# Tuned fp32 layer on one core: token rows split from the transposes' bank, another load order, memory rows in the second block, a reordered first block

## The chip, the cores and the metric

The kernel runs on one core of a Trainium2 chip. The metric is the device time in microseconds of that core. Its engines are named as the profile names them: PE (TensorE, matrix products and transposes), DVE (VectorE), ACT (ScalarE), POOL (GpSimd) and SP (SyncE, which issues the loads).

## The reference

One layer over 512 rows of 1024 numbers and 256 memory rows, all fp32: half a SwiGLU feed-forward, a mixer of three attentions with gates, and another half feed-forward.

```python
x = x + 0.5 * swiglu(rmsnorm(x, ffn1_norm), ffn1_wg, ffn1_wu, ffn1_wd)
h = rmsnorm(x, mix_norm)
aq, ak, av, bq, bk, bv, cq = split(h @ w_in)
o_a = diff_attention(rope(norm(aq)), rope(norm(ak)), av, lam)
o_b = chunk_band_attention(norm(bq), norm(bk), bv, b_rel_bias)
mk, mv = split(rmsnorm(mem, mem_norm) @ w_mem_kv)
o_c = memory_attention(norm(cq), norm(mk), mv)
y = sum over i of sigmoid(h @ w_gate + b_gate)_i * (o_i @ w_branch_i)
x = x + y @ w_out
x = x + 0.5 * swiglu(rmsnorm(x, ffn2_norm), ffn2_wg, ffn2_wu, ffn2_wd)
x = rmsnorm(x, final_norm)
```

D_FF is 2816; the memory attention (branch C) has 4 heads of 128.

## The kernel before

**Arithmetic.** Each fp32 operand is split (`split`, L75 to L78) into a high half, cast by ACT, and a low half, the difference, made by DVE; a product is three matmuls (high by high, low by high, high by low). Weights come by SP into one of six raw buffers ("raw", 128x1024) and are split from there.

**The feed-forward halves** go through the hidden columns in four chunks of 4, 6, 6 and 6 tiles of 128 (`CHUNKS`). Two tiles make an *item*. Gate and up projections of an item are computed by a scheme with seven block products instead of eight: operands on the token side are seven matrices `M[1]` to `M[7]` (split sums and differences of the transposed rows, made by `Operands.rows` and `combine`), on the weight side seven blocks, four of them plain weights or sums `s1` to `s4` of weights (`Item.prep`). A product (`mm7`) is 24 matmuls of 128x256 into an accumulator bank; between products that share a bank, ACT saves it (`snap`), DVE adds the saved part (`plus`, the tiles `cc`), ACT applies the silu (`sg`) and DVE multiplies (`pr`). `run_jobs` goes through a list of jobs; each job's weight block is prepared ahead as far as a ring of blocks has room, and PE runs the jobs in the order of the list, written out by hand. Behind an item's products comes the chunk's down-projection with 128x512 matmuls (L110 to L112): 96 in the first chunk, with the last two products of the chunk behind its first step.

**Rows.** The four row tiles of x are loaded, their mean squares are taken by ACT in two halves, POOL raises them to the power -1/2 (`rs`, L121), DVE scales them by it and by the gain (`xn`, L141), PE transposes eight squares into two "t" banks (L201), ACT copies each bank to a raw buffer (L202), and `combine` forms the operands from it. The 256 memory rows (two tiles `mt`) go the same way to `mT` (`mem_rows`, `norm_T`); in the program they stand ahead of FFN1's last chunk, but the scheduler puts their norms, and the first one's transposes (L149), in the first block.

**Start of the mixer.** The memory keys' product goes into the two "s" banks, then come `norm4` and `heads_T` (transposes of `mk`), the query product, and the memory values' product `mv`, again in the "s" banks. Then the attention steps run by a plan, a string in which `p` is a part of the next projection, `f` a part of the gates' product, `c.qt`, `c.sc`, `c.sc2`, `c.pt`, `c.pv` the steps of the memory attention (query transposes, scores of two pairs of heads, transposed probabilities, product with `mv`). The row maximum `nm` (L754) and the exponentials `p` (L759) stand behind each score; `yb` (L834) is a part of the rotary embedding, from tables that POOL scales (L687, L691), and `hb` (L697) is the gates' bias.

PE's order inside `run_jobs` is written by hand; the other engines' orders are set by the scheduler.

## Time and profile before

| | us |
|---|---|
| median of 3 runs | 1266.1 (1265.81 to 1266.46) |
| profiled execution, own time | 1268.73 |
| span of the profiled execution | 1266.9 |
| PE busy | 1228.1 |
| DVE busy | 843.0 |
| ACT busy | 596.8 |
| POOL busy | 106.2 |

The span is what the trace covers; the execution's own time has 1.8 us more around it. A share of busy time is a mean over the span; the rows below show the stretches apart.

### The profile page before, as it was taken

To read this page: it belongs to the slowest core of one execution; us is meant where nothing else is said; L and a number is where in the kernel's file an instruction comes from. 1 tells how busy PE (TensorE), PEld (TensorE's weight loads), DVE (VectorE), ACT (ScalarE), POOL (GpSimd) and SP (SyncE) were. 2 spreads that over 40 slices of the span, in tenths; PEclk is the share of its full clock that TensorE was granted. 3 is DMA by queue.
4 is the path that set the end of the run, shared out by engine and by line. 5 is a ranking of instruction groups with operands and counts; after the bars stand their busy time and mean duration, and the time that the engine had idled before them with its cause. 6 is when DMAs were issued, how large, how long until landed. Compare 5 with 4: busy or idle time off the path is not lost.

```text
span 1266.9 us, 19640 instructions
## 1 busy us (share of the span) xinstructions
PE 1228.1 (97%) x7808; PEld 1119.2 (88%) x7808; DVE 843.0 (67%) x1377; ACT 596.8 (47%) x1115; POOL 106.2 (8%) x108
## 2 busy tenths in 40 slices
PE   7889999999999899999999999999989999999997
PEld 7779989989987799999999999888887998998996
DVE  7977667667664756667765664554697776766753
ACT  7534525435443455554554544442464452542543
POOL 1100000000000301111121121111000000000002
PEclk8899999999999899999999999999989999999999
DMA  6532423323333413212221321145143242332311
GB/s 222 174 103 82 135 84 107 127 79 122 102 123 117 123 39 109 88 42 84 88 88 54 93 88 38 63 146 186 34 135 115 70 134 97 101 125 76 123 44 67
DMA packets 53084, 127.57 MB, mean 101 GB/s; under 512 B 10112, under 2 KB 10624, under 8 KB 52992
## 3 DMA queue, kind: packets, MB, share of 16 engines
q1 hardware_dynamic: 52416, 125.27, 31.1%
q8 instruction: 61, 1.00, 0.3%
q10 hardware_dynamic: 576, 1.05, 0.2%
q14 instruction: 31, 0.25, 0.1%
HBM read 122.11 MB, written 4.19 MB: 100 GB/s over the span
## 4 chain that ended last, share of the span: by engine, by line
PE 91%; DVE 4%; ACT 1%; DMA 1%; POOL 1%; issue 1%; SPq 0%; POOLq 0%; DVEq 0%; ACTq 0%
PE ps_s L373 19%; PE ps_g L110 9%; PE ps_g L112 9%; PE ps_g L111 9%; PE ps_o L373 5%; PE ps_p L110 5%; PE ps_p L112 5%; PE ps_p L111 4%; PE ps_p L373 4%; PE ps_g L373 4%; PE ps_s L110 3%; PE ps_s L111 3%; PE ps_s L112 3%; PE ps_o L906 2%; PE ps_s L874 2%; PE ps_t L722 1%
## 5 line engine op out<-in xcount | busy, mean ns | idle before, releaser
L77 ACT CAST whi<-wraw 128x1024 fp32r<-128x1024 f32 (+1 forms) x120 | 119.1, 993 | 144.6 <-PE ps_s L373 74.1
L78 DVE TENSOR_TENSOR wlo<-wraw,whi 128x1024 fp32r<-128x1024 f32 (+1 forms) x120 | 137.9, 1151 | 67.8 <-ACT whi L77 65.1
L373 PE MATMUL ps_s<-mhi,whi 128*128 128x256 f32 x496 | 140.3, 283 | 8.1 <-ACT snap L417 7.9
L373 PE MATMUL ps_s<-mlo,whi 128*128 128x256 f32 x496 | 139.3, 281 | 0.0
L373 PE MATMUL ps_s<-mhi,wlo 128*128 128x256 f32 x496 | 138.3, 281 | 0.6 <-DVE wlo L78 0.6
L373 PEld LDWEIGHTS ps_s<-mhi,whi 128*128 128x128 f32 x496 | 94.6, 191 | 10.6 <-ACT snap L417 9.5
L77 ACT CAST whi<-quarter 128x1024 fp32r<-128x1024 f32 x54 | 56.8, 1052 | 96.4 <-PE ps_o L112 22.4
L373 PEld LDWEIGHTS ps_s<-mlo,whi 128*128 128x128 f32 x496 | 94.7, 191 | 0.9 <-DVE mlo L78 0.2
L373 PEld LDWEIGHTS ps_s<-mhi,wlo 128*128 128x128 f32 x496 | 94.5, 191 | 0.9 <-DVE wlo L78 0.8
L110 PE MATMUL ps_p<-whi,hh 128*128 128x384 f32 (+1 forms) x264 | 95.0, 360 | 0.0
L112 PE MATMUL ps_p<-whi,hl 128*128 128x384 f32 (+1 forms) x264 | 89.6, 340 | 0.0
L111 PE MATMUL ps_p<-wlo,hh 128*128 128x384 f32 (+1 forms) x264 | 89.0, 337 | 0.0
L78 DVE TENSOR_TENSOR wlo<-quarter,whi 128x1024 fp32r<-128x1024 f32 x54 | 66.0, 1222 | 23.9 <-ACT whi L77 23.9
L110 PE MATMUL ps_g<-hh,fh 128*128 128x512 f32 x192 | 78.1, 407 | 0.0
L112 PE MATMUL ps_g<-hh,fl 128*128 128x512 f32 x192 | 75.5, 393 | 0.1
L111 PE MATMUL ps_g<-hl,fh 128*128 128x512 f32 x192 | 74.9, 390 | 0.0
L859 DVE CAST kx<-ps_t 128x256 fp32r<-128x256 f32 x32 | 13.6, 425 | 84.6 <-PE ps_t L857 84.6
L121 POOL TENSOR_TENSOR rsh<-msh,mhalf 128x4 f32<-128x4 f32 x38 | 45.2, 1191 | 277.5 <-DVE msh L127 225.8
L78 DVE TENSOR_TENSOR fl<-wraw,fh 128x768 fp32r<-128x768 f32 x48 | 50.0, 1042 | 24.0 <-ACT fh L77 24.0
L77 ACT CAST fh<-wraw 128x768 fp32r<-128x768 f32 x48 | 39.9, 833 | 37.7 <-PE ps_g L111 22.4
L724 ACT COPY pT<-ps_t 128x512 f32<-128x512 f32 (+3 forms) x56 | 23.5, 452 | 69.3 <-PE ps_t L722 69.3
L110 PEld LDWEIGHTS ps_p<-whi,hh 128*128 128x128 f32 x264 | 50.4, 191 | 1.6
(416 smaller groups left out, 3691.7 us busy)
## 6 DMA issues: line engine op xcount, KB each, us to landing
wraw<-in_ffn_w SPq DMA_DIRECT2D x88, 512.0 KB, 3.8
wraw<-in_ffn_wd SPq DMA_DIRECT2D x44, 512.0 KB, 3.9
wraw<-in_w_u SPq DMA_DIRECT2D x32, 384.0 KB, 3.2
wraw<-in_w_gb SPq DMA_DIRECT2D x32, 384.0 KB, 3.1
wraw<-in_w_gf SPq DMA_DIRECT2D x16, 384.0 KB, 3.1
wraw<-in_w_mem_kv SPq DMA_DIRECT2D x8, 512.0 KB, 4.1
wraw<-in_w_out SPq DMA_DIRECT2D x8, 512.0 KB, 4.8
x_sb<-in_x SPq DMA_DIRECT2D x4, 512.0 KB, 7.0
```

Source lines behind the costliest of these rows:

```text
L77: nc.scalar.copy(out=hi, in_=raw)
L78: (engine or nc.vector).tensor_tensor(out=lo, in0=raw, in1=f32(hi), op=ALU.subtract)
L110: nc.tensor.matmul(ps, lhsT=st[0], rhs=mv[0], start=first, stop=False)
L111: nc.tensor.matmul(ps, lhsT=st[0], rhs=mv[1], start=False, stop=False)
L112: return nc.tensor.matmul(ps, lhsT=st[1], rhs=mv[0], start=False, stop=last)
L121: nc.gpsimd.tensor_tensor(out=rs, in0=ms, in1=mhalf[:, :n], op=ALU.pow)
L373: nc.tensor.matmul(ps[:, c], lhsT=x, rhs=y, start=first and j + k + n == 0, stop=k == 3 and n == 2, skip_group_check=True)
L722: nc.tensor.transpose(ps[:, j * P:(j + 1) * P], pt[:, j * P:(j + 1) * P], ident)
L724: nc.scalar.copy(out=pT[:, :n * P], in_=ps[:, :n * P])
L859: nc.vector.tensor_copy(out=un.kx[:, :, qs], in_=heads(p2[:, 0:256], 2))
L874: nc.tensor.matmul(out_, lhsT=q, rhs=k, start=j == 0, stop=j == 1)
L906: nc.tensor.matmul(o[:, vs], lhsT=pT[:, j * P:(j + 1) * P], rhs=un.v[:, j, vs], start=j == 0, stop=j == i)
```

## The change

- x row tile 1 is loaded second, ahead of the gain.
- The first two row tiles' high and low halves are taken from the transposes' bank; ACT's copy to the raw buffer stands behind.
- The mean square of a row is one activation of 1024 instead of two of 512 (`mean_rsqrt` takes either).
- `run_jobs` is called over all chunks, up to the last down-projection half; the second chunk's first product is put behind the first chunk's last two (`hole`). The first block of each feed-forward has another order of products, with the fifth in two halves ("5a", "5b"); `s1`, `s2` and `s4` are made apart, when they are first needed.
- The accumulators of the second half of a down-projection stand in another order.
- The memory rows' loads, squares and norms stand at the end of the second chunk's jobs' list ahead of its down-projection (`mem_norms`, as `middle`), in raw buffers; their transposes stay where `mem_rows` was.
- At the start of the mixer the `mv` product goes into "t" banks, the transposes of `mk` come behind it, and the plan of the first projection tile (`PLAN_C0`) is another one.

```diff
-PLAN_C0 = "p2 c.qt p2 c.sc p2 f4 c.sc2 p3 f2 c.qt f2 c.pt f4 c.pv"
+PLAN_C0 = "p6 c.qt p3 f4 c.sc f4 c.sc2 f2 c.qt f1 c.pt f1 c.pv"
...
-                nc.scalar.copy(out=self.raw[dh][:, :, t * P:(t + 1) * P], in_=k4(ps))
-            self.combine(t)
+                cols = slice(t * P, (t + 1) * P)
+                if t < 2:
+                    split(k4(ps), *(v[:, :, cols] for v in self.M[1 + dh]))
+                nc.scalar.copy(out=self.raw[dh][:, :, cols], in_=k4(ps))
+            if t >= 2:
+                self.combine(t)
...
-        ss = tiny("ss", 2)
-        dump = scratch("sq")
-        for dh in range(2):
-            d = slice(dh * 512, dh * 512 + 512)
-            square_half(src[:, d], dump[:, d], ss[:, dh:dh + 1])
+        ss = tiny("ss", 1)
+        square_half(src, scratch("sq") if dump is None else dump, ss)
...
-        if t == 0:
+        if t == 1:
             gain1 = load_gain("ffn1_norm")
-        elif t < 3:
+        if 0 < t < 3:
             w1_raw.append(load(a["ffn1_w1"][0, t - 1], 1024))
...
+                if self.s1 is None:
+                    self.s1 = quarter()
+                    add(out=self.s1, in0=self.raw(2), in1=self.raw(3), op=ALU.add)
                 if p == 6:
-                    self.s1, self.s2 = quarter(), quarter()
-                    add(out=self.s1, in0=self.raw(2), in1=self.raw(3), op=ALU.add)
+                    self.s2 = quarter()
                     add(out=self.s2, in0=self.s1, in1=self.raw(0), op=ALU.subtract)
...
+                elif p == "5a":
+                    self.z = bank("p" if self.ft // 2 % 2 else "o")
+                    mm7(self.z, blk, 5, True, (0,))
+                elif p == "5b":
+                    mm7(self.z, self.blk5, 5, False, (1,))
...
                 order += [(items[0], 1), (items[0], 2), (items[1], 1), (items[1], 2)]
+                order += [(items[0], "5a"), (items[0], 6), (items[0], "5b"), (items[0], 7), (items[1], 6), (items[0], 4),
+                          (items[0], 3), (items[1], 5), (items[1], 7)]
             else:
-                order += [(items[0], 1), (items[0], 2)]
...
+                if n == 1:
+
+                    jobs.insert(hole, product(items[0], 1))
...
+            if n == 1 and middle:
+                jobs.append(Job(middle, lambda got: None, 0, 0))
...
-                    acc.extend(bank(t) for t in (("g", "g", "s", other) if dh == 0 else ("s", z, "g", "g")))
+                    acc.extend(bank(t) for t in (("g", "g", "s", other) if dh == 0 else (z, "g", "g", "s")))
...
+    def mem_norms():
+
+        gain = load(a["mem_norm"].partition_broadcast(P), 1024)
+        mix_in["mn"] = []
+        for t in range(NMT):
+            mt = load(a["mem"][t * P:(t + 1) * P, :], 1024)
+            xn = scratch("mn")
+            rs = mean_rsqrt(squares(mt, xn))
+            for dh in range(2):
+                norm_half(xn, mt, rs, (gain[:, :512], gain[:, 512:]), dh)
+            mix_in["mn"].append(xn)
...
-        gain = load_gain("mem_norm")
         for t in range(NMT):
-            mt = scratch("mt")
-            nc.sync.dma_start(out=mt, in_=a["mem"][t * P:(t + 1) * P, :])
-            norm_T(mt, squares(mt), gain, mix_in["mT"], t)
+            for dh in range(2):
+                transpose_half(mix_in["mn"][t], *mix_in["mT"], t, dh)
...
-        yn = mem_pool.tile([P, 512], F32, tag="mk", name="mk", bufs=3)
-        sq = mem_pool.tile([P, 512], F32, tag="mk", name="mksq", bufs=3)
-        heads_T(norm4(mk_ps[t], yn, sq, gck), mkT, slice(t * P, (t + 1) * P))
+        yn = mem_pool.tile([P, 512], F32, tag="mk", name="mk", bufs=2)
+        sq = mem_pool.tile([P, 512], F32, tag="mksq", name="mksq", bufs=2)
+        mk.append(norm4(mk_ps[t], yn, sq, gck))
...
-    mv_ps = rows_product([bank("s") for _ in range(NMT)], mT, a["w_mem_kv"], 512, **mem_w)
+    mv_ps = rows_product([bank("t") for _ in range(NMT)], mT, a["w_mem_kv"], 512, **mem_w)
     mv = base.tile([P, NMT, 512], F32, tag="kx", name="mv", bufs=2)
     for t in range(NMT):
         nc.scalar.copy(out=mv[:, t, :], in_=mv_ps[t])
+    for t in range(NMT):
+        heads_T(mk[t], mkT, slice(t * P, (t + 1) * P))
```

The instructions stand in another order on the engines. DVE in FFN1's first block, before the change; `mt` is a memory row tile, `mlo` and `wlo`, `olo`, `flo` are low halves of tokens and of weight blocks, `quarter` a sum of weights, and the last row is the low half of item 1's sixth product's block:

```order
L141 SCALAR_TENSOR_TENSOR xn<-mt,rs,gain 128x512 x2
L78 TENSOR_TENSOR wlo<-quarter,whi 128x1024
L78 TENSOR_TENSOR wlo<-wraw,whi 128x1024
L399 TENSOR_TENSOR quarter<-wraw 128x1024
L78 TENSOR_TENSOR wlo<-quarter,whi 128x1024
L400 TENSOR_TENSOR quarter<-quarter,wraw 128x1024
L409 TENSOR_TENSOR quarter<-wraw 128x1024
L78 TENSOR_TENSOR olo<-quarter,ohi 128x1024
L422 TENSOR_TENSOR cc<-ps_o,snap 128x512
L405 TENSOR_TENSOR quarter<-wraw,quarter 128x1024
L78 TENSOR_TENSOR flo<-quarter,fhi 128x1024
```

DVE at the same place after it; the last row is again the low half of item 1's sixth product's block:

```order
L78 TENSOR_TENSOR flo<-quarter,fhi 128x1024
L243 TENSOR_TENSOR gl<-gl,quarter 128x4x256
L78 TENSOR_TENSOR mlo<-quarter,mhi 128x4x128
L78 TENSOR_TENSOR mlo<-gh,mhi 128x1024
L78 TENSOR_TENSOR wlo<-quarter,whi 128x1024
L442 TENSOR_TENSOR pr<-sg,cc 128x256
L403 TENSOR_TENSOR quarter<-wraw 128x1024
L78 TENSOR_TENSOR mlo<-gl,mhi 128x1024
L406 TENSOR_TENSOR quarter<-quarter,wraw 128x1024
L418 TENSOR_TENSOR quarter<-wraw 128x1024
L414 TENSOR_TENSOR quarter<-wraw,quarter 128x1024
L78 TENSOR_TENSOR wlo<-quarter,whi 128x1024
```

The memory rows' half norms (`xn<-mt`) have gone from this stretch, and item 1's sums of weights (L403, L406) stand just ahead of the block that needs them.

PE in FFN1's first block, before, where products 5 (`ps_o<-mhi,whi`) and 6 (`ps_s<-mhi,ohi`) of item 0 begin, each in its bank; L149 are the transposes of the first memory row:

```order
L373 MATMUL ps_g<-mhi,flo 128x256
L373 MATMUL ps_o<-mhi,whi 128x256
L373 MATMUL ps_s<-mhi,ohi 128x256
L149 MATMUL ps_t<-ident,xn 128x128 x8
L373 MATMUL ps_o<-mlo,whi 128x256
L373 MATMUL ps_o<-mhi,wlo 128x256
L373 MATMUL ps_o<-mhi,whi 128x256
```

PE after, in the second chunk, where the first memory row's transposes (`mn`) stand:

```order
L376 MATMUL ps_p<-mhi,ohi 128x256
L376 MATMUL ps_p<-mlo,ohi 128x256
L376 MATMUL ps_p<-mhi,olo 128x256
L149 MATMUL ps_t<-ident,mn 128x128 x8
L376 MATMUL ps_s<-mhi,whi 128x256
L376 MATMUL ps_s<-mlo,whi 128x256
L376 MATMUL ps_s<-mhi,wlo 128x256
```

The transposes have moved from between two products of the first block to between two products of the second chunk.

DVE at the start of the mixer, before, around the first row maxima of scores (L754):

```order
L78 TENSOR_TENSOR fl<-wraw,fh 128x768
L754 TENSOR_REDUCE nm<-ps_g 128x2
L78 TENSOR_TENSOR fl<-wraw,fh 128x768
L679 TENSOR_SCALAR gb<-gb 128x64
L755 TENSOR_SCALAR nm<-nm 128x2
L754 TENSOR_REDUCE nm<-ps_g 128x2
L697 TENSOR_SCALAR hb<-hb 128x24
L755 TENSOR_SCALAR nm<-nm 128x2
L820 TENSOR_REDUCE hss<-squ 128x4
L834 TENSOR_TENSOR yb<-ps_p,sg 128x4x32 x2
```

DVE there after the change (L793 is the maximum `nm`, L736 `hb`, L873 `yb`, L859 the sum of squares for the rotary part's norm):

```order
L78 TENSOR_TENSOR mkl<-ps_t,mkh 128x4x128
L78 TENSOR_TENSOR cql<-ps_t,cqh 128x512
L736 TENSOR_SCALAR hb<-hb 128x24
L859 TENSOR_REDUCE hss<-squ 128x4
L873 TENSOR_TENSOR yb<-ps_p,sg 128x4x32 x2
L875 TENSOR_TENSOR y_4321<-ps_p,cg 128x256
L127 TENSOR_SCALAR msh<-hss 128x4
L876 TENSOR_TENSOR y_4321<-y_4321,yb 128x256
L879 TENSOR_TENSOR y_4321<-y_4321,rsh 128x256
L883 TENSOR_TENSOR hl_4328<-y_4321,hl_4328 128x4x64
L793 TENSOR_REDUCE nm<-ps_g 128x2
L794 TENSOR_SCALAR nm<-nm 128x2
```

`hb`, the sum of squares, `yb` and the rotary sums have moved from behind the first two maxima to ahead of the first.

## Rows read from the trace of the kernel before

**Rows 1.** The page, part 4: the chain that ended last, shares by engine.

```profile
PE 91%; DVE 4%; ACT 1%; DMA 1%; POOL 1%; issue 1%; SPq 0%; POOLq 0%; DVEq 0%; ACTq 0%
```

**Rows 2.** Waits of PE: what released it, us in total, times, longest.

```profile
PE ps_s L373 <- ACT snap L417: 7.9, 8, 1.5
```

**Rows 3.** Windows: length, busy of PE, PEld, DVE, ACT, POOL, PEclk, DMA share, GB/s.

```profile
40.00:50.00 10.00, 8.46 (x57) 8.05 (x57) 9.56 (x12) 6.29 (x10) 1.39 (x1) 0.84 0.52 173
100.00:150.00 50.00, 50.00 (x427) 49.63 (x426) 37.31 (x44) 27.70 (x39) 0.00 (x0) 1.00 0.36 114
415.00:420.00 5.00, 5.00 (x13) 3.93 (x14) 3.84 (x9) 1.20 (x2) 1.80 (x2) 0.54 0.21 72
```

**Rows 4.** DMA issues at 1.16 and at 1.64 us: count, KB, us to landing.

```profile
gain<-in_ffn_norm SPq DMA_DIRECT2D x1, 512.0 KB, 5.2
x_sb<-in_x SPq DMA_DIRECT2D x1, 512.0 KB, 6.2
```

**Rows 5.** Timeline of DVE, first block: start, duration, line, operation [idle before it].

```profile
23.31 1.22 DVE L78 TENSOR_TENSOR flo<-wraw,fhi 128x1024 fp32r<-128x1024 f32 x1
24.45 0.69 DVE L221 TENSOR_TENSOR quarter<-gl,gh 128x512 f32<-128x512 f32 x1
25.05 1.22 DVE L400 TENSOR_TENSOR quarter<-quarter,wraw 128x1024 f32<-128x1024 f32 x1
...
34.91 1.42 DVE L141 SCALAR_TENSOR_TENSOR xn<-mt,rs,gain 128x512 f32<-128x512 f32 x2 [0.44 <-POOL rs L121]
...
55.45 1.22 DVE L78 TENSOR_TENSOR flo<-quarter,fhi 128x1024 fp32r<-128x1024 f32 x1
```

**Rows 6.** Timeline of POOL, first block.

```profile
9.58 0.55 POOL L121 TENSOR_TENSOR rs<-ms,mhalf 128x1 f32<-128x1 f32 x1 [3.09 <-DVE ms L193]
...
30.02 4.86 POOL L121 TENSOR_TENSOR rs<-ms,mhalf 128x1 f32<-128x1 f32 x1 [9.81 <-DVE ms L156]
```

**Rows 7.** Timeline of PE, first block of FFN1.

```profile
35.81 1.94 PE L149 MATMUL ps_t<-ident,xn 128*128 128x128 f32 x8 [1.23 <-DVE xn L141]
38.12 0.58 PE L373 MATMUL ps_o<-mlo,whi 128*128 128x256 f32 x1 [0.36 <-DVE mlo L78]
...
64.71 0.39 PE L373 MATMUL ps_s<-mhi,whi 128*128 128x256 f32 x1 [1.51 <-ACT snap L417]
64.94 0.28 PE L373 MATMUL ps_s<-mlo,whi 128*128 128x256 f32 x1
...
67.45 0.28 PE L373 MATMUL ps_s<-mhi,wlo 128*128 128x256 f32 x1
...
97.31 0.39 PE L110 MATMUL ps_g<-whi,gh 128*128 128x512 f32 x1
...
97.99 0.28 PE L373 MATMUL ps_s<-mhi,whi 128*128 128x256 f32 x1
```

**Rows 8.** Timeline of PE, start of the mixer.

```profile
414.92 0.77 PE L110 MATMUL ps_s<-mwh,mh 128*128 128x512 f32 x1 [5.78 <-DVE mk L602]
...
438.22 0.39 PE L110 MATMUL ps_g<-mkh,cqh 128*128 128x256 f32 x1 [0.74 <-ACT p L759]
...
450.56 0.34 PE L110 MATMUL ps_p<-whi,hh 128*128 128x384 f32 x1
```

**Rows 9.** Timeline of DVE, start of the mixer.

```profile
424.20 1.21 DVE L78 TENSOR_TENSOR mwl<-wraw,mwh 128x1024 fp32r<-128x1024 f32 x1
...
439.85 0.17 DVE L697 TENSOR_SCALAR hb<-hb 128x24 f32<-128x24 f32 x1
```

**Rows 10.** Timeline of POOL, start of the mixer.

```profile
438.43 0.87 POOL L691 TENSOR_TENSOR sg<-sg,ga 128x128 f32<-128x128 f32 x2
```

**Rows 11.** Timeline of PE, first block of FFN2.

```profile
928.85 0.58 PE L373 MATMUL ps_o<-mlo,whi 128*128 128x256 f32 x1 [3.17 <-DVE mlo L78]
...
986.33 0.28 PE L373 MATMUL ps_s<-mhi,whi 128*128 128x256 f32 x1
```

**Rows 12.** Timeline of DVE, first block of FFN2.

```profile
943.67 1.23 DVE L78 TENSOR_TENSOR flo<-quarter,fhi 128x1024 fp32r<-128x1024 f32 x1
```

More of the change, by code (lines that the diff above doesn't have):

```diff
@@ L362, in block, with mm7 @@
             return weight(None, 1024, fp, (("fhi", "flo"), ("ohi", "olo"))[n - 4], 1, raw=raw)
[L364 to L366 removed]
+        def mm7(ps, blk, m, first, parts=(0, 1)):
+            for j in parts:
                 c = slice(j * HS, (j + 1) * HS)
@@ L435, in done @@
             def done(self, f):
+                if not self.G:
+                    self.G += [fp.tile([P, 6, S], F32R, tag=t, name=t) for t in ("gh", "gl")]
                 split(self.pr[f], *(v[:, self.g0 + f, :] for v in self.G))
@@ L1084, in row_out @@
     def row_out(t, ss):
-        ms = tiny("ms", 1)
-        nc.vector.tensor_scalar(out=ms, in0=ss[:, 0:1], scalar1=EPS, scalar2=ss[:, 1:2], op0=ALU.add, op1=ALU.add)
-        rs = rsqrt(ms)
+        rs = mean_rsqrt(ss)
         xn = scratch("xn")
```

94 lines of the change are left out of this document (50 added, 44 removed).

## The prediction

> **What bounds the kernel now.** I read the page first, then the sum of TensorE's (PE's) waits, then the timelines of the stretches where PE waits. PE is on 91% of the chain that ended last [rows 1], so the reader is to look only for what shortens or lengthens PE's own row of work. Between 100 and 150 us PE is busy 50.00 of 50 [rows 3], and it stays so through the other chunks; its waits lie at three places. One kind is the wait for the snapshot copy, 7.9 us in eight pieces [rows 2], spread over the first blocks of both feed-forward halves. The first block of FFN1 is held by the vector engine (DVE): it works back to back from 20 to 60 us, PE stands at 38.12 for a low half, at 64.71 for a snapshot (1.51), and PE's mark "first product of the next chunk" comes at 97.99 [rows 5, 7]. The start of the mixer has the longest single wait, 5.78 us for `mk`, at 414.92 [rows 8]. The first block of FFN2 has a 3.17 us wait at 928.85, and its mark comes at 986.33 [rows 11]. Each pause is paid twice: after the 5.78 us the granted clock was 0.54 of full speed over 415 to 420, thus near the lower of the two levels (1.2 of 2.4 GHz), and 5 x 0.46 = 2.3 us of PE's work were lost; the 40 to 50 us stretch, with short pauses, shows 0.84, 10 x 0.16 = 1.6 us lost [rows 3]. These two are my prices, 1.6 and 2.3, for one pause of some two us or more.
>
> The profiled execution's span is 1266.9 us and its own time 1268.73; the median of the runs is 1266.1. I add up the terms against the span and put the sum on the median, so 1266.1 plus the sum.
>
> **Unit prices.** A product is 24 matmuls of 128x256; from its second at 64.94 to its last at 67.45 are 22 steps of 0.114, so 2.74 us for a product. A 512-wide matmul of the down-projection takes (97.99 - 97.31) / 3 = 0.227 [rows 7]. On DVE, back to back, a 1024-wide operation takes 24.45 - 23.31 = 1.14, a 512-wide one 0.60 [rows 5], and a 256-wide one, by the same scale, an estimated 0.34.
>
> **Term 1, FFN1's first block: -5.1.** Removed from it: both memory rows' norms, two each of a mean, two half norms (34.91, 1.42) and a 0.44 us wait for POOL in front [rows 5]; DVE does nothing else then. Moved behind it: the second operands of the products that now come later (s2, s4 are computed one at a time), and the order of products, so that DVE comes earlier to the block of item 1's sixth product. Row tile 1 comes second and the gain third: the gain now lands about where x row 1 landed, 1.64 + 6.2 = 7.8, instead of 1.16 + 5.2 = 6.4 [rows 4]. That puts row 0's norm some 1.4 later, but the first two rows' low halves no longer wait for raw copies, and rows 2 and 3 land where they did. I leave the fourth row's norm where it ended before, at 22.1 (the next 1024-wide operation began 1.14 ahead of 23.31). From there the changed order has, up to and with the low half of item 1's sixth product, 19 operations of 1024, eight of 512 and two of 256: 21.6 + 4.8 + 0.7 = 27.1, with 1.1 of idle time while ScalarE casts `ohi`: 50.3. Before, the same low half ended at 55.45 + 1.22 = 56.7 [rows 5]. From there PE has seven products and the down-projection's 96 matmuls ahead of the mark: 7 x 2.74 + 96 x 0.227 = 19.2 + 21.8, so 91.3. The two snapshot waits of 1.5 are not among it, because products 4 and 3 of item 0 now lie between the sixth product's snapshot and the next user of its bank. PE has run out of work by about 48.1, so it pauses about two us and I add the lower price of a clock fall, 1.6: 92.9 against 97.99, -5.1. Bounds: without a pause -6.7; if DVE's chain starts 2 us later (the gain holds row 0 and all behind it), -3.
>
> **Term 2, the memory rows in the second block: +1.3.** Their transposes stood in a pause of PE (eight in 1.94 at half clock, at 35.81 [rows 7]) and cost nothing; the work that hid them was DVE's. They now stand in a chunk in which PE never waits: half of 1.94, so +1.0. PE takes them in its order, whether the norm is there or not. On SP's queue a gain and two memory rows come to stand between the `w1` loads and the first `wd` loads of that chunk, in three of the six raw buffers, and the `wd` loads behind them wait for those buffers. By the changed order the norm is ready 13.2 to 14 us after the block's start and PE arrives after 13.6, +0.3. DVE has room, 37.31 of 50 us busy [rows 3]; the norms' own time, 1.42 each, costs nothing by itself. Bounds: +0.8 to +2.5 without the rival below.
>
> A row that speaks against this part: POOL's power operation of one column took 0.55 at 9.58, and 4.86 at 30.02, while DVE worked without a gap [rows 6]. The Trainium skill, "SBUF — State Buffer", section "SBUF: two separate sides", says that a DVE operation with two SBUF inputs and a GpSimd operation that reads SBUF exclude each other for a whole instruction; the row agrees with it in kind. By that rule the moved norm would meet the same lock beside the second chunk's subtractions; it is case (c) below.
>
> **Term 3, start of the mixer: -0.7.** The `mv` product leaves the "s" banks, in which it waited for `mk`, for "t" banks that are free: the 5.78 and the 2.3 lost on the clock go. What is late next, in order: the second pair's low half now stands behind four reductions on DVE (some 1.7); the second `mk` transpose waits for a "t" bank, that is for ScalarE's copy of `mv`, which stands behind a table load (some 1.2, unshown before, bounds 0 and 2); the first query transposes wait for `mkl` (2 to 3.7). Last comes the second score: its bank's exponentials follow the row maximum `nm`, and on DVE `hb` and `yb` now stand ahead of `nm` (before: `nm` first, then `hb` at 439.85 [rows 9]). `hb` and the rope tables are small loads on SP's queue behind the weight loads that wait for the last low half of `mv` (before, the one at 424.20 and one more right behind it [rows 9], 426.6; now some 421.9), so they come 4.7 us earlier: POOL's last table operation, before 438.43 + 0.87 = 439.3 [rows 10], ends at 434.7, and the maxima and exponentials of the first score about 440.0. The second score, before at 438.22, is then at 440; from it to the second projection tile there are 27 matmuls of 512, 384 or 256 columns and 20 transposes, now without the six of a projection and twelve of the gates that the new plan puts earlier: 8.3 us, so 448.3 against 450.56 [rows 8], -2.3. The idle time ahead of the second score costs a clock fall, +1.6. Bounds: +1.5 where two of the new waits fall together, -5.2 where the table chain doesn't bind (8.1 less 1.7 and 1.2).
>
> **Term 4, FFN2's first block: +1.9.** There are no memory rows to take out here. DVE has as much to do; the copies to the raw buffer now follow the subtraction that reads the same bank (0.7 to 1.2 of DVE waits at the third row). By the list the low half of item 1's sixth product is done at 944.95, before at 943.67 + 1.23 = 944.9 [rows 12], but before PE had products 4 and 3 of item 0 to do meanwhile and now it has not: it pauses from about 941.5. Mark: 944.95 + 19.2 + 21.8 = 985.95, and the clock fall at the higher price, 2.3: 988.2 against 986.33, +1.9. Bounds -0.5 (no fall) and +2.5.
>
> **The rest: 0.** The one job list over all chunks, the hole that takes the next chunk's first product into the down-projection, the other order of accumulators and the squares in one activation of 1024 lie where PE has no wait before; PE's work covers them. If that cover fails at one boundary it costs one low half, 1.2.
>
> **Sum.** -5.1 + 1.3 - 0.7 + 1.9 = -2.6: 1263.5 us, -0.21%. A measurement of this kernel can tell some 0.2% (2.5 us) from no change: faster means below 1263.6, slower above 1268.6.
>
> **The rivals.** (a) More gain: the table chain does not bind the second score and the pause at the mixer's start goes whole, term 3 is -5.2, the sum -5.1 + 1.3 - 5.2 + 1.9 = -7.1: 1259.0. For it: `nm` needs only scores; the chain is four engines long and my times for SP and POOL are placed by hand. Against: `hb` and `yb` stand ahead of `nm` in DVE's order. (b) No change, the first block does not do what it is written to do: row 1 second delays the gain, the DVE list starts 2 us late, term 1 is -3, and a new wait makes term 3 +0.5: -3 + 1.3 + 0.5 + 1.9 = +0.7, 1266.8. (c) Slower: the norm of the first memory row is late in FFN1's second block, because POOL's power operation takes 4.86 instead of 0.55 beside a busy DVE [rows 6]. PE, in order, stands at the transposes for 4.3, and the clock falls: term 2 is 1.3 + 4.3 + 2.3 = 7.9, the sum -5.1 + 7.9 - 0.7 + 1.9 = +4.0, 1270.1. It decides from about 4 us of lateness. For it: the 4.86. Against: DVE has gaps there, a quarter of its time [rows 3].
>
> **How the numbers follow.** Forecast 0.50, spread from 1261 to 1265.5 by its terms' bounds; (a) 0.25; (b) 0.14; (c) 0.11. Of the forecast's 0.50, 0.28 lies below 1263.6. Faster 0.28 + 0.25 = 0.53, same 0.22 + 0.14 = 0.36, slower 0.11. The range leaves out (c) and a small tail of (a): 1257.5 to 1267.5.
>
> **What would show it.** Right: the low half of item 1's sixth product ends near 50, the next chunk's down-projection mark moves by some 5 us, no 5.78 wait at 409 to 415, the wait ahead of the second score names `nm` or an exponential. Wrong: a PE wait of over 1 us for `xn` or `mn` in FFN1's second block; a first product that starts after 18 us; the second projection tile later than 450.6 less what term 1 and 2 gave; any new wait at a chunk boundary.

## Result: 1273.8 us, slower by 0.6%

The changed kernel's median is 1273.82 us over 4 runs (1272.23 to 1275.16), beside 1266.1 over 3 runs of the kernel before: ratio 1.0060 [1.0041, 1.0080]. Forecast were 1263.5, with a range of 1257.5 to 1267.5. The time is outside it and the sign is wrong. A fourth run of the kernel before took 1740.59 us and is left out.

The profiled execution took 1272.23, its span is 1270.3. On the page PE is still nearly the whole chain that ended last (before 91% [rows 1]), with DVE up from the rest. From the section of the page on the chain, shares by engine:

```profile
PE 90%; DVE 6%; ACT 1%; DMA 1%; issue 1%; POOL 0%; SPq 0%; POOLq 0%; DVEq 0%; ACTq 0%
```

The sum of PE's waits in the kernel after (engine, line, what it waited for: us in total, times, longest) against [rows 2]: the snapshot's 7.9 us are no longer at the head; other waits have come instead.

```profile
PE ps_o L376 <- DVE mlo L78: 5.6, 2, 3.6
PE ps_g L110 <- ACT gh L77: 4.0, 2, 2.0
PE ps_t L206 <- ACT gh L210: 3.8, 1, 3.8
```

To see where the time went I cut each trace into six stages, at starts of PE's rows: FFN1's first block up to the next chunk's first product (where that product already stands in the first block's down-projection, 2.72 us are taken off, so 97.40 - 2.72 = 94.7 in the first trace of after); FFN1's second chunk; its third and fourth; from there to FFN2's first transposes (the mixer); FFN2's first block; its three other chunks. The two marks in the first trace of after, each with the product that is taken off in front of it (before: 97.99 [rows 7] and 986.33 [rows 11]):

```profile
97.40 0.28 PE L376 MATMUL ps_g<-mhi,whi 128*128 128x256 f32 x1
991.18 0.28 PE L376 MATMUL ps_g<-mhi,whi 128*128 128x256 f32 x1
```

Two traces of each kernel:

| stage, us | before | before, again | after | after, again | mean difference |
|---|---|---|---|---|---|
| FFN1, first block | 98.0 | 97.2 | 94.7 | 97.0 | -1.8 |
| FFN1, second chunk | 91.05 | 91.05 | 92.6 | 93.05 | +1.8 |
| FFN1, third and fourth | 184.4 | 184.4 | 185.0 | 185.1 | +0.65 |
| mixer | 531.8 | 531.2 | 530.35 | 530.1 | -1.3 |
| FFN2, first block | 81.1 | 80.5 | 85.8 | 85.7 | +4.95 |
| FFN2, other chunks | 273.6 | 273.65 | 275.0 | 275.1 | +1.4 |

The differences sum to +5.7, the spans' own difference (mean 1271.6 against 1265.95). So FFN1's first block gave 1.8 and not 5.1, the mixer 1.3; all the rest lost. A single trace is good to a few us in a first block: g1, g2 and h2 below have PE, DVE and ACT in the same order in FFN2's first block, and their traces have 83.1, 86.3 and 86.9 us for it. FFN1's third and fourth chunk and FFN2's later ones repeat to 0.1.

### The profile page after: what moved, and what is told of

It reads as the page before. It is cut to its first block, busy times and chain, and to the rows that moved or that the text cites. A ratio compares the mean times of both kernels' runs of the same rounds, so it can differ in the third digit from the quotient of the medians.

```text
span 1270.3 us, 19631 instructions
## 1 busy us (share of the span) xinstructions
PE 1230.0 (97%) x7808; PEld 1120.4 (88%) x7808; DVE 845.7 (67%) x1377; ACT 598.3 (47%) x1103; POOL 106.2 (8%) x108
## 4 chain that ended last, share of the span: by engine, by line
PE 90%; DVE 6%; ACT 1%; DMA 1%; issue 1%; POOL 0%; SPq 0%; POOLq 0%; DVEq 0%; ACTq 0%
PE ps_s L376 18%; PE ps_g L110 9%; PE ps_g L112 9%; PE ps_g L111 9%; PE ps_o L376 5%; PE ps_p L110 5%; PE ps_p L112 5%; PE ps_p L111 5%; PE ps_p L376 4%; PE ps_g L376 4%; PE ps_s L112 2%; PE ps_s L110 2%; PE ps_s L111 2%; PE ps_o L945 2%; PE ps_s L913 2%; PE ps_t L761 1%
## 5 line engine op out<-in xcount | busy, mean ns | idle before, releaser
L376 PE MATMUL ps_s<-mlo,whi 128*128 128x256 f32 x512 | 145.4, 284 | 2.1 <-DVE mlo L78 2.1
L376 PE MATMUL ps_s<-mhi,whi 128*128 128x256 f32 x512 | 145.7, 285 | 1.9 <-ACT whi L77 1.6
L376 PE MATMUL ps_s<-mhi,wlo 128*128 128x256 f32 x512 | 145.3, 284 | 2.0 <-DVE wlo L78 2.0
L376 PEld LDWEIGHTS ps_s<-mhi,whi 128*128 128x128 f32 x512 | 99.5, 194 | 2.9 <-ACT whi L77 1.8
L376 PEld LDWEIGHTS ps_s<-mlo,whi 128*128 128x128 f32 x512 | 98.8, 193 | 3.3 <-DVE mlo L78 2.9
L376 PEld LDWEIGHTS ps_s<-mhi,wlo 128*128 128x128 f32 x512 | 99.3, 194 | 2.4 <-DVE wlo L78 2.4
```

The lines of the kernel that those rows point to most:

```text
L376: nc.tensor.matmul(ps[:, c], lhsT=x, rhs=y, start=first and j + k + n == 0, stop=k == 3 and n == 2, skip_group_check=True)
```

## Experiments

Each edit is shown against the kernel named ahead of it. "Ratio" is to the kernel before, in the same set of runs on one chip, with its 95% interval; its own median was 1265.9 to 1267.1 in the five sets, so kernels of different sets are compared by their ratios (0.1% is 1.27 us). The theory at the start was that the changed order of products is at fault, in FFN2's first block above all; the rivals were the hand-fixed list over all chunks, the memory rows' new place, the new mixer start, and the first rows' loads and their split from the bank.

### One part undone in the kernel after

**The same kernel again.**

> The changed kernel once more, beside the kernel before on the same chip. Theory A (the loss lies in FFN2's first block and at the second down-projection step of the first chunks): about +6 to +8 us against before in the median, and the profile again shows FFN2's first block some 4 to 5 us longer than before and a 2.0 us wait for gh in both halves. Rival B (the first trace was an unlucky one, what differs is the number of falls of the granted clock): the trace shows other falls, and the FFN2 block differs from the first trace by over 1.5 us.

1274.77, ratio 1.0059 [1.0044, 1.0074]: the same loss.

**e1: FFN2's first block in the old order.**

```diff
+                if pre == "ffn2":
+                    order += [(items[0], 6), (items[0], 5), (items[0], 7), (items[0], 4), (items[0], 3),
+                              (items[1], 6), (items[1], 5), (items[1], 7)]
+                else:
```

> The changed kernel with FFN2's first block in the order of products of the kernel before (6, 5, 7, 4, 3, 6, 5, 7), all else as changed. Theory A1 (the new order of products is what costs FFN2's block time): 2 to 4 us less than the changed kernel, and the waits at the second item's sixth product (1.6 and 1.7 us) go. Rival A2 (VectorE sets that block's end, TensorE only comes to it earlier, and the order is not the cause): within 1 us of the changed kernel, the waits merely stand elsewhere.

1271.53, ratio 1.0047 [1.0030, 1.0063], not resolved from after's 1.0059. In its trace the block went from 85.8 to 82.7, not to the 80.5 to 81.1 of before; the waits of 1.6 and 1.7 are gone, and one for a low half is now 4.67.

**e2: the first chunks' last two products ahead of the down-projection instead of behind its first step.**

```diff
+                    if n == 0 and dh == 0:
+                        jobs += end
                     for k in range(0, nf, 2):
...
                         if dh == 0 and k == 0:
-                            jobs += end
+                            if n > 0:
+                                jobs += end
```

> The changed kernel with the first chunks' last two products (4 and 3 of the second item) ahead of the down-projection's first step instead of behind it, so that this step and the next chunk's first product both stand between product 3 and the step that reads its result. Theory A: the two waits of 2.0 us for gh go, -3 to -4 us. Rival: the weight blocks of products 4 and 3 come late instead, since they are prepared later than TensorE wants them; the time is within 1 us of the changed kernel and new waits for whi or wlo of 1.5 us or more show.

1270.93, ratio 1.0033 [1.0023, 1.0042], by the ratios 3.3 less than after, as forecast; the two waits for `gh` are gone. First blocks 95.8 and 84.5.

**e7: both edits.**

> The two edits of e1 and e2 together: FFN2's first block in the old order of products, and the first chunks' last two products ahead of the down-projection. If the two causes are apart, their gains add up: 6 to 7 us less than the changed kernel, +0.5 to +1.5 against the kernel before. If VectorE sets FFN2's first block whatever TensorE's order (rival), the second adds only FFN1's half: 4 to 5 us less, +3 against before.

1272.05, ratio 1.0042 [1.0028, 1.0056]: no better than e2 alone. FFN2's block is at 86.1, with PE waits for the snapshot of 2.59 and 1.51 again and one of 5.76 for a low half. The gains don't add here; in the trace other waits stand where those that were taken away had been.

**e4: the old mixer start and plan.** (The old `PLAN_C0`, `mv` in the "s" banks, `heads_T` of each `mk` tile right behind its norm.)

> The changed kernel with the start of the mixer as before (the value product in the s banks, key transposes ahead of it, the old plan of the first projection tile). If the changed start gives what the trace suggests (-1.4 us from the end of the key product to the second projection tile): 1 to 2 us slower than the changed kernel, with the 5.8 us wait back. Rival (the clock fall it now has in another place takes the gain away): the same as the changed kernel within 0.7 us.

1275.64, ratio 1.0069 [1.0054, 1.0084], unresolved from after; in the trace the mixer takes 533.1 instead of 530.1.

**e3: the memory rows back ahead of the last chunk.** They then run in FFN1's first block, as before.

```diff
+        gain = load_gain("mem_norm")
         for t in range(NMT):
-            for dh in range(2):
-                transpose_half(mix_in["mn"][t], *mix_in["mT"], t, dh)
+            mt = scratch("mt")
+            nc.sync.dma_start(out=mt, in_=a["mem"][t * P:(t + 1) * P, :])
+            norm_T(mt, squares(mt), gain, mix_in["mT"], t)
...
-    ffn("ffn1", x_sb, ops, fp, row_mix, raws=w1_raw, before_last=mem_rows, middle=mem_norms)
+    ffn("ffn1", x_sb, ops, fp, row_mix, raws=w1_raw, before_last=mem_rows)
```

> The changed kernel with the memory rows' loads, squares and norms back where they were (the first block decides, as the scheduler puts them), all else as changed. From the traces FFN1's second chunk is 1.6 to 2.0 us longer since the change, while its first block ends 1 to 3 us earlier. Theory (a trade of two about equal sums): within 1 us of the changed kernel; first block 2 to 4 us later, second chunk 1 us shorter, since VectorE sets the first block's end and gets the norms' 3.8 us back. Rival (TensorE has pauses in the first block that hide the norms): 1 to 2 us faster than the changed kernel.

1277.39, ratio 1.0084 [1.0066, 1.0102]. FFN1's first block 104.15, 7 to 9.5 longer than with the rows moved; its second chunk 91.9, 0.7 to 1.2 shorter. (The median moved by 3 only, since FFN2's first block came out shorter, 83.9, without an edit of its own.) The move of the memory rows is a gain in that block, so something else there costs about as much as the move gives.

**e6: one job list for each chunk, no hole.** (`run_jobs(jobs, RING)` at the end of each chunk, PE's order fixed by hand job by job, new order of products kept.)

> The changed kernel with the job list as before: one list per chunk, TensorE's order fixed job by job and interleaved by the scheduler, no hole. The first block's order of products, the memory rows and the mixer stay as changed. Theory (the one hand-fixed list costs two waits of 2.0 us for gh, and 0.15 to 0.6 us in each later chunk through longer steps of the matmuls, 0.1178 instead of 0.1134, some 2.5 in all): 3 to 5 us less than the changed kernel, and FFN2's second to fourth chunk take 91.1, 91.5 and 91.1 us as before, not 91.7, 91.8 and 91.5. Rival (the carried list pays for itself at the chunk ends, the longer steps come from elsewhere): within 1 us of the changed kernel, and the later chunks stay as long.

1276.02, ratio 1.0077 [1.0062, 1.0092]: not better. But the later chunks are back at their old times: 184.4 and 273.7 (91.95 in FFN1's second, which holds the moved transposes). So the one list costs some 0.9 + 0.65 + 1.4 = 2.9 us there. In e6's trace the first blocks and the mixer are longer instead (97.7, 87.4 and 532.5), and the time shows no gain.

### All order undone, then the rest part by part

**g1: e6 with the old order of products and of accumulators.** What is left of the change: loads, split from the bank, single squares, memory rows' place, mixer start.

```diff
-                order += [(items[0], "5a"), (items[0], 6), (items[0], "5b"), (items[0], 7), (items[1], 6), (items[0], 4),
-                          (items[0], 3), (items[1], 5), (items[1], 7)]
+                order += [(items[0], 6), (items[0], 5), (items[0], 7), (items[0], 4), (items[0], 3),
+                          (items[1], 6), (items[1], 5), (items[1], 7)]
...
-                    acc.extend(bank(t) for t in (("g", "g", "s", other) if dh == 0 else (z, "g", "g", "s")))
+                    acc.extend(bank(t) for t in (("g", "g", "s", other) if dh == 0 else ("s", z, "g", "g")))
```

> The changed kernel with the order of products of both first blocks, the job lists (one per chunk, job by job) and the accumulators' order as before; kept are the load order, the split from the bank, the single squares, the memory rows in the second chunk and the new start of the mixer. Theory B (the order of products and the hand-fixed list are what loses; the kept edits gain some 1.3 us at the mixer and 2 to 3 in FFN1's first block less 1 in its second chunk): 2 to 4 us faster than before, 1262 to 1264.5. Rival (the kept edits gain nothing with the old order, since TensorE's pauses hid the memory rows' norms there): within 1.5 us of before or slower.

1271.65, ratio 1.0042 [1.0027, 1.0058]. This refutes the theory that the order alone is at fault: with all of it undone the kernel is still 5.5 us slower than before, and FFN1's first block ends at 99.7.

**g2: g1 with the memory rows back (e3's edit).**

> g1 with the memory rows' norms back in the first block. If they are worth moving with the old order: FFN1's first block 2 to 4 us later than in g1, its second chunk 0.9 to 1.2 us shorter, the time 1 to 3 us above g1. Rival: the first block as in g1, the time 1 us below g1.

1274.51, ratio 1.0065 [1.0042, 1.0088]; first block 103.7, second chunk 91.05. By these two stages the move is worth 4.0 less 0.9 here (2.9 by the ratios, whose intervals overlap); it isn't the fault either.

**g4: g1 with the old mixer start (e4's edit).**

> g1 with the start of the mixer as before. From the traces the new start gives 1.3 us against before up to the second projection tile (FFN1's end to FFN2's first transposes 530.2 against 531.5). Theory: 1 to 2 us above g1. Rival: the same as g1 within 0.5 us, the wait of 5.8 us replaced by others of the same sum.

1270.78, ratio 1.0034 [1.0021, 1.0047]; mixer 530.0 with the old start and 530.0 with the new one. Beside the old lists the new start shows no gain.

**g3: g1 with the first rows as before: gain second, split from the raw copies.**

```diff
-                cols = slice(t * P, (t + 1) * P)
-                if t < 2:
-                    split(k4(ps), *(v[:, :, cols] for v in self.M[1 + dh]))
-                nc.scalar.copy(out=self.raw[dh][:, :, cols], in_=k4(ps))
-            if t >= 2:
-                self.combine(t)
+                nc.scalar.copy(out=self.raw[dh][:, :, t * P:(t + 1) * P], in_=k4(ps))
+            self.combine(t)
...
+            if t < 2:
+                part(1, r0[:, :, cols], cols)
+                part(2, r1[:, :, cols], cols)
+                return
...
-        if t == 1:
+        if t == 0:
             gain1 = load_gain("ffn1_norm")
-        if 0 < t < 3:
+        elif t < 3:
```

> g1 with the first two row tiles taken from the raw copies again and the gain loaded second. The changed load order brings the gain 1.4 us later and the split from the bank makes the second tile's transposes wait for ScalarE's copy (3.8 us at 13.8 us in the trace of the changed kernel). Theory (these two cancel): within 0.7 us of g1. Rival (the split makes the first product earlier, 15.6 against 16.4, and this reaches the end): g1 faster by 0.8 or more. Other rival (the wait for the copy reaches the end, in FFN2 too): g3 faster by 1 or more.

1261.22, ratio 0.9960 [0.9946, 0.9974], and once more below: 10.4 less than g1 by the ratios, where the theory had the two cancel, and faster than both kernels. Its FFN1 block ends at 92.7; 92.9 was the mark that I had forecast for the whole change.

### Split or loads?

**h1: g1 with the old split only (g3's first two pieces). h2: g1 with the old loads only (g3's last piece).**

> g1 with the rows' split from the raw copies as before, but x row 1 loaded second and the gain third as changed. Theory S (the split from the bank is the loser: the raw copy waits for VectorE's subtraction, the bank comes free late, row tiles 2 and 3 are transposed behind the first product, and their operands are late): close to g3, FFN1's first block ends at 92.5 to 94.5 and FFN2's takes 80 to 81, 1261 to 1263. Rival L (the late gain is the loser): FFN1's first block ends at 97 or later, 1266 or more.

> g1 with the gain loaded second as before, the split from the bank kept. Theory S: FFN1's first block ends at 97 to 100, FFN2's takes 83, 1269 to 1272. Rival L: FFN1's first block ends at 93 to 95, FFN2's takes 83, 1263 to 1265.

| median, us | split from the bank | split from the raw copy |
|---|---|---|
| row 1 loaded second | g1 1271.65 | h1 1262.45 |
| gain second, as before | h2 1266.61 | g3 1261.22 |

Ratios: h1 0.9966 [0.9953, 0.9979], h2 0.9997 [0.9987, 1.0006]. By the ratios the split from the bank costs 9.6 with the new loads (1.0042 - 0.9966) and 4.7 with the old; the loads cost 0.8 with the raw copy and 5.7 with the split. So it is the split, and the new loads, which cost little or nothing alone, make it twice as dear. The first blocks of FFN1 and FFN2, one trace each (g3 two):

| FFN1, FFN2, us | split from the bank | split from the raw copy |
|---|---|---|
| row 1 loaded second | g1 99.7, 83.1 | h1 93.0, 80.3 |
| gain second, as before | h2 93.8, 86.9 | g3 92.7, 80.3; 92.3, 81.7 |

h1 came as theory S has it. h2 fits neither: its FFN1 block ends where rival L has it, and its time lies between the two. In FFN1's block the great loss needs both edits; with the old loads the split costs 1.1 to 1.5 there (PE's wait for the copy is there too, 2.85 at 11.53), and h2's loss stands in FFN2's block, where no row is loaded. How much of that is the spread of one trace is open.

The mechanism, in DVE's and ACT's rows of after at the first row tile (start, us; duration, engine, line, operation, out<-in):

```profile
12.43 1.28 DVE L78 TENSOR_TENSOR mlo<-ps_t,mhi 128x512 fp32r<-128x512 f32 x2
```

```profile
13.15 0.59 ACT L210 COPY gh<-ps_t 128x512 f32<-128x512 f32 x1
13.74 0.59 ACT L210 COPY gl<-ps_t 128x512 f32<-128x512 f32 x1
```

Two subtractions read the two "t" banks from 12.43 to 13.71, and ACT's copies stand behind them, one by one. That two engines may not be in one bank at a time is also what the Trainium skill says ("PSUM — Partial Sum Buffer", section "PSUM bank collisions raise a hardware error": ScalarE's read with VectorE's read included); the rows agree as to the order. What follows from this order is the price: a "t" bank is now free only after DVE, which has other work in front, and then ACT. PE in the kernel after, at the second tile's transposes:

```profile
13.79 1.97 PE L206 MATMUL ps_t<-ident,xn 128*128 128x128 f32 x8 [3.84 <-ACT gh L210]
15.58 0.58 PE L376 MATMUL ps_s<-mhi,whi 128*128 128x256 f32 x1
...
22.70 1.04 PE L206 MATMUL ps_t<-ident,xn 128*128 128x128 f32 x8
...
26.17 1.03 PE L206 MATMUL ps_t<-ident,xn 128*128 128x128 f32 x8
```

The first product starts no later for it (16.35 before, 15.58 after). What comes late are the third and fourth tile (22.70 and 26.17; before from 15.61 and 23.00), whose transposes need the same banks once more. PE's rows of g1, then of g3:

```profile
14.62 1.97 PE L206 MATMUL ps_t<-ident,xn 128*128 128x128 f32 x8 [3.84 <-ACT gh L210]
16.41 0.58 PE L376 MATMUL ps_s<-mhi,whi 128*128 128x256 f32 x1
...
23.09 1.03 PE L206 MATMUL ps_t<-ident,xn 128*128 128x128 f32 x8
...
38.59 0.58 PE L376 MATMUL ps_o<-mlo,whi 128*128 128x256 f32 x1 [2.18 <-DVE mlo L78]
...
99.73 0.28 PE L376 MATMUL ps_s<-mhi,whi 128*128 128x256 f32 x1
```

```profile
15.40 1.09 PE L206 MATMUL ps_t<-ident,xn 128*128 128x128 f32 x4 [3.19 <-DVE xn L141]
16.50 1.05 PE L206 MATMUL ps_t<-ident,xn 128*128 128x128 f32 x4
...
35.20 0.58 PE L376 MATMUL ps_o<-mlo,whi 128*128 128x256 f32 x1 [2.64 <-DVE mlo L78]
...
92.73 0.28 PE L376 MATMUL ps_s<-mhi,whi 128*128 128x256 f32 x1
```

In g3 the third tile is transposed at 15.40 and 16.50, around the first product's first matmul; in g1 its banks are not free then (the second tile's last copy ends at 20.14 + 0.60), and it comes at 23.09, behind the first product and the start of the second. DVE's first step of the sums for the third and for the fourth tile, in g1 and in g3:

```profile
26.36 0.68 DVE L225 TENSOR_TENSOR gh<-gh 128x512 f32<-128x512 f32 x1
...
31.23 0.69 DVE L225 TENSOR_TENSOR gh<-gh 128x512 f32<-128x512 f32 x1
```

```profile
19.37 0.69 DVE L225 TENSOR_TENSOR gh<-gh 128x512 f32<-128x512 f32 x1
...
25.84 0.68 DVE L225 TENSOR_TENSOR gh<-gh 128x512 f32<-128x512 f32 x1
```

They are 7.0 and 5.4 later (26.36 - 19.37, 31.23 - 25.84). DVE, which makes the low halves that PE waits for, is short of input meanwhile: from 20 to 28 it is busy 6.34 us of 8 in g1, 7.56 in g3:

```profile
20.00:28.00 8.00, 8.00 (x67) 8.00 (x67) 6.34 (x8) 3.47 (x7) 1.46 (x1) 0.93 0.01 2
```

```profile
20.00:28.00 8.00, 8.00 (x69) 8.00 (x68) 7.56 (x10) 4.58 (x8) 0.47 (x1) 0.96 0.01 2
```

(Views by window, g1 and g3: from:to and length, busy us and count of PE, PE's weight loads, DVE, ACT, POOL, then granted clock, DMA share, GB/s.) The low half for which PE stands comes 3.4 later (38.59 against 35.20), and the block's end 7.0 later. These 7.0 are not the third tile's handed on: PE's lag is 3.4 at the low half, 4.2 and 5.8 at the last two snapshot waits (64.71 and 70.83 against 60.53 and 65.04), and from 64 to 72 the granted clock is 0.79 in g1, 1.00 in g3. What adds the second half is not shown.

**i1: g1 with the second tile in two other banks, so that the "t" banks wait for one tile only.**

```diff
-                ps = bank("t")
+                ps = bank("t" if t != 1 else "po"[dh])
```

> g1 (old order and lists, changed loads, split from the bank), but the second row tile is transposed into the banks p and o, which are idle then, instead of the two t banks. If the split costs by holding the t banks until ScalarE's copy: the 3.84 us wait for the copy goes, FFN1's first block ends at 92.5 to 95 instead of 99.6, FFN2's takes 80 to 82, and the time comes to 1262 to 1264.5. Rival (it costs by the copies and subtractions standing later in the engines' queues, whatever the bank): the wait moves and the time stays at 1269 to 1272.

1264.69, ratio 0.9991 [0.9982, 1.0000], just above what was expected: by the ratios 6.5 of g1's 10.4 over g3 are back, with the split from the bank kept. PE's rows: the 3.84 wait is gone, the first product starts 2.9 earlier than in g1, the low half is there at 34.59, the block ends at 95.14.

```profile
11.58 0.66 PE L206 MATMUL ps_p<-ident,xn 128*128 128x128 f32 x4 [0.83 <-DVE xn L141]
13.49 0.39 PE L376 MATMUL ps_s<-mhi,whi 128*128 128x256 f32 x1 [0.59 <-ACT mhi L77]
...
34.59 0.58 PE L376 MATMUL ps_o<-mlo,whi 128*128 128x256 f32 x1 [0.97 <-DVE mlo L78]
...
45.26 0.39 PE L376 MATMUL ps_s<-mhi,whi 128*128 128x256 f32 x1 [2.69 <-ACT snap L426]
...
95.14 0.28 PE L376 MATMUL ps_s<-mhi,whi 128*128 128x256 f32 x1
```

DVE's first steps of the sums for the third and fourth tile in i1:

```profile
23.70 0.69 DVE L225 TENSOR_TENSOR gh<-gh 128x512 f32<-128x512 f32 x1
...
24.91 0.68 DVE L225 TENSOR_TENSOR gh<-gh 128x512 f32<-128x512 f32 x1
```

That the hold of the "t" banks is most of the price, beside the new loads, is so shown; beside the old loads it was not tried. It is not the third tile alone, which is still 4.3 later than in g3 (23.70 against 19.37): the fourth is not late (24.91 against 25.84), and PE has its low half as early as in g3 (34.59 and 35.20). Of the 2.4 that are left in this block 2.0 stand as a longer wait for a snapshot (2.69 at 45.26; in g3 0.67 at 44.20), whose cause is not settled.

**g3 again.**

> g3 once more in five rounds: 4 to 6 us faster than before (ratio 0.995 to 0.997). Rival (g3's first result was a favourable draw of the clock falls): within 2.5 us of before.

1261.07, ratio 0.9962 [0.9948, 0.9975].

### Is the new order of products right once the rows are?

**h3: after with the old rows and loads (g3's edit). h4: the same with e6's list for each chunk, new order kept.**

> The changed kernel with nothing but the rows' split and the load order as before. If the split costs the same under the changed order: 6 to 10 us less than the changed kernel, 1264 to 1268. If the changed order hides it (VectorE's list to item 1's sixth product ended at 50.6 there, as forecast): within 3 us of the changed kernel, and order and list are the losers in their own right.

> h3 with a job list per chunk, fixed job by job as before: the new order of products with the old machinery. The later chunks get shorter by the 2.7 us that the longer steps cost (91.05, 91.5, 91.05 in FFN2). If the new order itself gains in FFN1's first block: 1258 to 1261, faster than g3. If it loses: 1263 to 1267.

h3 1271.39, ratio 1.0030 [1.0019, 1.0042]; h4 1270.57, ratio 1.0030 [1.0015, 1.0044]. Some 4 us less than after: h3 is near its second case, h4 slower than both of its own. So there are two faults, each of which hides the other: by the ratios order and lists alone cost 8.9 (h3 against g3), rows and loads alone 10.4 (g1 against g3), both together 12.7. The first is the order of products (or of accumulators, which these runs don't part from it) and not the list: h4, with lists by chunk, has the same ratio as h3, its FFN1 block at 95.8 (g3 92.7 and 92.3), FFN2's at 84.6 (80.3 and 81.7). In FFN1 beside the split the new order looks like a gain (99.7 in g1, 97.7 in e6, 94.7 and 97.0 in after).

## Why the prediction was wrong, step by step

**Two steps failed: one without a number, and the cover that I gave PE.** The first: "the first two rows' low halves no longer wait for raw copies" stands in term 1 without a price. I took the split by the copy that it takes off DVE's path and not by the bank. I asked who waits for ACT's copy, and not who frees the "t" bank and whose transposes need it next; the fourth row's norm did end where I left it (20.73 + 1.41 = 22.1), the transposes came late. Term 4 names the copies that follow the subtraction, as waits of DVE, and has nothing for them in its sum. By the ratios the price is 4.7 beside the old loads and 9.6 beside the new, with the old order and lists; in the kernel after, rows and loads undone give 3.8 (h3). The second is the new order of products: term 1 and term 4 have one pause each and PE at work for the rest. By the ratios order and lists cost 8.9 beside the old rows (h3 against g3). Under "the rest: 0" the one job list's cover failed in every later chunk: 2.9 us by the stages, where I allowed 1.2 at one boundary, though lists by chunk win no time back (e6, h4).

By the stages, the 8.3 us between the forecast -2.6 and the measured +5.7 are 3.3 in term 1, 0.5 in term 2, -0.6 in term 3, 3.05 in term 4 and 0.65 + 1.4 in the rest. In h3, without the split and the new loads, FFN1's first block is no shorter (96.25, against 94.7 and 97.0) and FFN2's is (82.5, against 85.8 and 85.7).

**Term 1, -5.1, came as -1.8.** (-3.3 and -0.3 by the two pairs of traces.) The sign is right. DVE's list is forecast almost exactly: the low half of item 1's sixth product, forecast to end at 50.3, ends at 49.38 + 1.22 = 50.6 in after.

```profile
49.38 1.22 DVE L78 TENSOR_TENSOR wlo<-quarter,whi 128x1024 fp32r<-128x1024 f32 x1
```

What failed is the step from there to the mark, "seven products and the down-projection's 96 matmuls": 50.6 + 41.0 is 91.6, and the mark is at 94.7 and 97.0. PE's long waits are two. The one at 37.76, for a low half, lies ahead of this step; the one at 80.40, for `gh`, lies in it, where before it was 0.46, at 84.14. One product now stands between product 3 and the matmuls that read its result. I read the wait as the chain of `cc`, `sg`, `pr` and the cast, longer than that product; in e2, which puts the down-projection's first step there too, it is gone. The row of before, then those of after:

```profile
84.14 0.50 PE L110 MATMUL ps_g<-fhi,gh 128*128 128x512 f32 x1 [0.46 <-ACT gh L77]
```

```profile
37.76 0.58 PE L376 MATMUL ps_o<-mlo,ohi 128*128 128x256 f32 x1 [3.63 <-DVE mlo L78]
80.40 0.51 PE L110 MATMUL ps_g<-ohi,gh 128*128 128x512 f32 x1 [2.02 <-ACT gh L77]
```

The size of -5 is there, but for another edit: with the old order and the old rows the block goes from 98.0 and 97.2 to 92.7 and 92.3 (g3), with the memory rows' move and the single squares, and with the new order 3 of it are lost again (h3 96.25, h4 95.8).

**Term 2, +1.3: right in size, +1.8 in the stage.** The moved transposes cost 0.9 (91.95 in g1, 91.05 in g2), where I had 1.0, and the other 0.9 go with the one list; PE runs through them without a pause:

```profile
125.54 0.28 PE L376 MATMUL ps_p<-mhi,olo 128*128 128x256 f32 x1
125.65 1.04 PE L149 MATMUL ps_t<-ident,mn 128*128 128x128 f32 x8
126.45 0.37 PE L376 MATMUL ps_s<-mhi,whi 128*128 128x256 f32 x1
```

**Term 3, -0.7: -1.3 in the traces.** The 5.78 for `mk` [rows 8] is gone; the three waits forecast in its place are there, 1.51 at 412.89 (`mwl`, forecast 1.7), 1.07 at 425.60 (`mv`'s copy, 1.2) and 2.64 at 428.89 (`mkl`, 2 to 3.7). No wait stands ahead of the second score: the table chain did not bind, contrary to my step, and yet the pause was not won, for beside the old lists old and new start take the same time (g1, g4). Beside the new list e4's trace has the old start 3.0 longer, but its time is not resolved from after.

```profile
425.60 0.66 PE L651 MATMUL ps_t<-ident,mk 128*128 128x128 f32 x4 [1.07 <-ACT mv L688]
428.89 0.90 PE L651 MATMUL ps_t<-ident,y_sb 128*128 128x128 f32 x3 [2.64 <-DVE mkl L78]
```

**Term 4, +1.9: +4.95.** The direction was right, and the pause that I forecast is there (products 4 and 3 no longer fill the wait for the sixth: 1.62 and 1.68), but it is not alone: five waits came, where before had 3.17 at 928.85 [rows 11] and snapshots. PE's rows of after:

```profile
922.74 0.58 PE L376 MATMUL ps_g<-mhi,flo 128*128 128x256 f32 x1 [2.65 <-DVE flo L78]
...
929.01 0.51 PE L376 MATMUL ps_o<-mlo,ohi 128*128 128x256 f32 x1 [2.00 <-DVE mlo L78]
...
940.65 0.39 PE L376 MATMUL ps_s<-mhi,whi 128*128 128x256 f32 x1 [1.62 <-ACT whi L77]
...
942.84 0.58 PE L376 MATMUL ps_s<-mhi,wlo 128*128 128x256 f32 x1 [1.68 <-DVE wlo L78]
...
974.18 0.50 PE L110 MATMUL ps_g<-ohi,gh 128*128 128x512 f32 x1 [2.02 <-ACT gh L77]
```

From 920 to 945 DVE is busy 25.00 of 25 us and PE 17.05, at a granted clock of 0.82; before, DVE was as full (24.89) and PE had 21.08. After, then before:

```profile
920.00:945.00 25.00, 17.05 (x107) 16.36 (x107) 25.00 (x27) 16.08 (x21) 0.00 (x0) 0.82 0.35 119
```

```profile
920.00:945.00 25.00, 21.08 (x154) 20.45 (x153) 24.89 (x27) 17.54 (x22) 0.00 (x0) 0.86 0.38 119
```

So it is not that DVE has more to do, but that PE finds less to do meanwhile. The order undone gives 82.7 (e1), the split undone 82.5 (h3): each takes some 3 off the 85.8 in one trace, and how the two share it is open. Over the whole block, 916 to 1004, PE is busy 77.90 us against 81.31 before, and the granted clock is 0.94 against 0.96; I had counted one clock fall and no more idle time.

**The rivals.** (c) had the right sign and a near size, +4.0 against +7.5, but not by its mechanism. POOL's power operation for the first memory row takes 0.55; the second is slow, 3.47, and PE does not yet need it:

```profile
121.57 0.55 POOL L121 TENSOR_TENSOR rs<-ms,mhalf 128x1 f32<-128x1 f32 x1 [100.87 <-DVE ms L159]
124.93 3.47 POOL L121 TENSOR_TENSOR rs<-ms,mhalf 128x1 f32<-128x1 f32 x1 [2.82 <-DVE ms L159]
```

(a) was right that the table chain does not bind, but its time was not won. (b) named the first block, with the loads as its cause: they cost 0.8 with the raw copy, within the intervals, and 5.7 beside the split, which (b) doesn't have. Of the marks that I named as proof against me, a first product after 18 us did not come (15.58), and a new wait at a chunk's end did (2.02 for `gh`, at 80.40 and 974.18); it was the third and fourth tile's transposes that I should have named.

## What to carry to other kernels

Who reads a bank last decides when it is free: an edit that takes a copy off one engine's path can put the bank's release behind another, busier engine, so for each bank draw in its next writer and count from there (here the transposes of the tiles behind, whose sums begin 7.0 and 5.4 us later). Where a change has several parts, test each with the others undone: here two parts cost 9 and 10 us alone and 12.7 together, so that either, undone in the presence of the other, seemed to matter less than it does, and hid a gain of 5 us (1261.2 against 1266.1). The memory rows' move is likely the larger part of it (4.0 us of the first block in g2, beside the split; beside the old rows it was not tried). And an edit with no number in the sum deserves bounds like any other.

## What the runs showed of the hardware

**Two lengths of PE's step.** In the later chunks PE has no wait of over 0.12 us, before or after, and the loss there is that a matmul step of 256 columns is longer over a stretch of each chunk. Rows of before and of after at the same time in FFN2's second chunk, where the granted clock is 1.00 in both:

```profile
1011.90 0.28 PE L373 MATMUL ps_s<-mhi,flo 128*128 128x256 f32 x1
...
1014.28 0.28 PE L373 MATMUL ps_s<-mhi,flo 128*128 128x256 f32 x1
```

```profile
1011.90 0.28 PE L376 MATMUL ps_g<-mhi,wlo 128*128 128x256 f32 x1
...
1014.26 0.28 PE L376 MATMUL ps_s<-mlo,fhi 128*128 128x256 f32 x1
```

Between them lie 21 steps in before, 2.38 / 21 = 0.113, and 20 in after, 2.36 / 20 = 0.118, 4% more. Both kernels have both lengths, and in two traces of each they change over at the same places of this chunk, in after later than in before. Lists made chunk by chunk (e6, h4, g1) bring back the shorter chunks. What sets the length stays open.

**The clock differs between executions of one program.** Two traces of after, the same stretch, with 0.99 and 0.75 as the granted clock; FFN1's first block ends 2.3 apart:

```profile
45.00:50.00 5.00, 5.00 (x45) 5.00 (x44) 5.00 (x5) 3.37 (x4) 0.00 (x0) 0.99 0.12 25
```

```profile
45.00:50.00 5.00, 5.00 (x35) 5.00 (x34) 5.00 (x6) 2.94 (x4) 0.00 (x0) 0.75 0.10 15
```

Both pause shortly before (0.54 at 41.23, 0.54 at 41.66). So one trace's mark in a block with pauses is good to a few us only, and medians of several runs decide (after's own runs lie 3 us apart).
